# Token-major value products, and six gates and six outputs of the merge's third branch, as pairs of 512 and 256 columns

## The chip, the cores and the metric

One core of one Trainium2 chip. The metric is the device time of one execution, in microseconds (us), on that core. The parts named here are TensorE (PE: matmuls, and PEld: weight loads), VectorE (DVE), ScalarE (ACT), GpSimd (POOL) and SyncE (SP, whose queue issues nearly all DMAs), the on-chip memory SBUF and the matmul accumulators PSUM.

## The reference

Two layers over 256 tokens of width 1024. Each layer is a SwiGLU FFN, a mixer and a second SwiGLU FFN, each behind an RMS norm and added to the residual stream; a norm ends the program. The mixer projects the normed input once and feeds three branches, which a gated merge adds up:

```python
h = rms_norm(x, mix_norm[l])
proj = h @ w_in[l]
gm_u, gm_v, r_q, r_k, r_v, r_g, n_q, n_kv, n_g = jnp.split(proj, splits, axis=-1)
y_a = gmlp_mixer(jax.nn.gelu(gm_u), jax.nn.gelu(gm_v), ...)
y_b = retention_mixer(r_q, r_k, r_v, r_g, ...)
y_c = nsa_mixer(n_q, n_kv, n_g, ...)
g_a, g_b, g_c = jnp.split(jax.nn.sigmoid(h @ w_merge_gate[l] + b_merge_gate[l]), N_MIXERS, axis=-1)
mix = g_a * (y_a @ w_branch_out[l, 0]) + g_b * (y_b @ w_branch_out[l, 1]) + g_c * (y_c @ w_branch_out[l, 2])
x = x + mix @ w_o[l]
```

All data is float32.

## The kernel before

**Splits.** Every large product is done with operands split in two parts, a rounded high part and the rest (low), both of type float32r: high by high, high by low and low by high are accumulated in PSUM. Weights come in pieces of 512 KB through `issue` (lines 197 to 216): SP's queue loads a piece (`raw`, 3 buffers), ScalarE casts it to the high part (line 210), and VectorE and GpSimd subtract to get the low part (line 214), GpSimd taking a share of the columns. The two parts lie in one tile `hl` (4 buffers), so that `wk[k]` is a block of 128 rows with its high and low columns side by side. `piece` (line 220) hands a piece to a product and issues up to AHEAD = 2 pieces further.

**Two ways to multiply.** Feature-major products (features on the output's partitions, 256 tokens along its columns) hold the weight in the array. `mm_feat` (line 231) issues three matmuls of 256 columns for each block of 128 rows ("a step"). `mm_wide` (line 254) issues two for the same step: the weight's high part by the activations' high and low parts side by side, 512 columns into a whole PSUM bank, then its low part by the high activations, 256 columns added to the first half. The bank then holds two halves that have yet to be added. The first FFN product does so for most tiles (its halves are added after a copy by ScalarE, lines 391 and 392), and the second FFN product and the output product do so for seven of eight (they add both halves to x, line 374). Token-major products (tokens on the partitions) hold the activations in the array: `mm_tok` (line 269) issues three matmuls of 256 columns for each step, for one half of the tokens.

**Order.** TensorE's order is the order in which the program writes its matmuls; the products are generators that yield after each step, and `run_sides` lets side jobs (attention units, retention, gmlp, compression) write their instructions in between, when a condition holds or when an estimate of TensorE's time, `clk`, has gone on by so much. The other engines' queues are ordered by the tile framework when the program is built, and its waits are placed there too.

**The mixer** (`mixer`, line 489) runs: four feature-major tiles of keys and values, the token-major keys' and gates' product of 280 columns, queries, retention's queries and keys, then the token-major products that the change touches. `tok` (line 869) is called four times with two pieces of four steps of 256 columns: twice for the gMLP's values (`gv_evac`, line 797) and twice for the retention's values (`f_vr`, line 939). Each call fills one PSUM bank "mm" (2 buffers), one half of the tokens after the other, and then evacuates both halves with two ScalarE copies scaled by the tokens' norm factor `st["r"]`, line 800 or 942. After the second call for the gMLP a side job, `gv_norm` (line 805), applies gelu (`gelu2`, lines 455 to 461: squares and tanh on ScalarE, two VectorE steps at 459 and 461 per token half) and a layer norm. After the second call for the retention's values, `retention` (line 734) goes on: its products with the values wait for line 942. Meanwhile `unit` (line 616) computes attention: score matmuls from the "sc" banks (3 buffers), maxima on VectorE (645, 648), exponentials on ScalarE (650), scaling of P (652 to 655), transposes on TensorE (149).

**The merge.** Gates and branch outputs of branches a and b are done for eight tiles (lines 997 to 1009), interleaved with attention. Then branch c: gates two tiles at a time (`gates`, line 978: one "mm" bank for two gates, multiplication by the norm factor R at line 984, tanh on ScalarE at 987), outputs two tiles at a time (`outs`, line 990, four steps each, one "sc" bank), their gated product at line 1034 on VectorE, its addition to the other branches on GpSimd (1035), and the split of the merged tiles into high and low (`split_mix`, 1016 on ScalarE and 1017 on VectorE) for the output product, which starts with two tiles interleaved (`mm_pair`, line 1051) and needs the merged tiles in order. The last two outputs (d = 6) are done one tile at a time, with their own additions on VectorE (1043, 1045).

Of the kernel before, what the change touches and what calls it, by code (L numbers as in the profile page):

```python
# [9 lines left out]
AF = mybir.ActivationFunctionType  # L10
# [50 lines left out]
def tile_hybrid_block(  # L61
# [48 lines left out]
    def t2(tag="t2", bufs=6):  # L110
        return act.tile([128, 512], F32, tag=tag, name=nm(tag), bufs=bufs)
# [4 lines left out]
    def pmm():  # L116
        return ps.tile([128, 512], F32, tag="mm", name=nm("mm"), bufs=2)

    def psc():
        return ps.tile([128, 512], F32, tag="sc", name=nm("sc"), bufs=3)  # L120
# [17 lines left out]
    def mm(o, lhsT, rhs, start, stop):  # L138
        nc.tensor.matmul(o, lhsT=lhsT, rhs=rhs, start=start, stop=stop)  # L139
        n = 1  # L140
        for d in rhs.shape[1:]:
            n *= d
        if lhsT.dtype == F32R:
            clk[0] += max(n / 2400.0, 0.107) + 0.0025
        else:
            clk[0] += max(4 * n / 2400.0, 0.214)
# [73 lines left out]
    def piece(kn, n, cuts=1, between=None, ahead=AHEAD):  # L220
        if between:
            issue(cuts, between)
        i = used[0]
        while len(queue) < len(specs) and len(queue) <= i + ahead:
            issue({1: 4, 2: 2}.get(len(queue), 1))
        used[0] += 1
        assert specs[i] == (kn, n)
        r, queue[i] = queue[i], None
        return r
# [24 lines left out]
    def mm_wide(o, wk, ak, first, last):  # L254

        n = len(wk)
        for i in range(n):
            mm(o.rearrange("p (a b) -> p a b", a=2), lhsT=wk[i][:, 0], rhs=ak[i], start=first and i == 0, stop=False)
            mm(o[:, 0:256], lhsT=wk[i][:, 1], rhs=ak[i][:, 0], start=False, stop=last and i == n - 1)
            yield  # L260
# [8 lines left out]
    def mm_tok(o, wk, ak, half, first, last):  # L269

        n = len(wk)
        t = slice(half * 128, half * 128 + 128)
        for i in range(n):
            wh, wl = wk[i][:, 0], wk[i][:, 1]
            ah, al = ak[i][:, 0], ak[i][:, 1]
            mm(o, lhsT=ah[:, t], rhs=wh, start=first and i == 0, stop=False)
            mm(o, lhsT=ah[:, t], rhs=wl, start=False, stop=False)
            mm(o, lhsT=al[:, t], rhs=wh, start=False, stop=last and i == n - 1)
            yield


# [81 lines left out]
    def when_scaled(st, f):  # L363
        if "R" in st:
            f()
        else:
            st["q"].append(f)
# [121 lines left out]
    def mixer(l, st, nxt):  # L489
# [304 lines left out]
        u2 = {}  # L794
        vl = []

        def gv_evac(c):
            def f(p):
                for h in range(2):
                    S.activation(vls[:, 512 * h + c * 256:512 * h + c * 256 + 256], p[:, h * 256:h * 256 + 256], AF.Copy, scale=st["r"][:, h:h + 1])  # L800
                if c:
                    side(gv_norm())
            return f

# [64 lines left out]
        def tok(cuts, n, f):  # L869
            if n > 256:  # L870
                ps_ = [psc(), pmm()]
                k = 0
                for m in cuts:
                    wk = piece(m, n)
                    for i in range(m):
                        for h in range(2):
                            yield from mm_tok(ps_[h][:, 0:n], wk[i:i + 1], a[k:k + 1], h, k == 0, k == 7)
                        k += 1
                for h in range(2):
                    when_scaled(st, lambda h=h: f(h, ps_[h]))  # L880
            else:
                wk = []
                for i, m in enumerate(cuts):
                    wk += piece(m, n, ahead=min(AHEAD, 3 - i))
                p = pmm()
                for h in range(2):
                    yield from mm_tok(p[:, h * n:h * n + n], wk, a, h, True, True)
                when_scaled(st, lambda: f(p))

        def f_c(i, o):  # L890
            for n in range(2):
# [45 lines left out]
            ev.add("kr")  # L937

        def f_vr(c):
            def f(p):  # L940
                for h in range(2):
                    S.activation(vr[h][:, c * 256:c * 256 + 256], p[:, h * 256:h * 256 + 256], AF.Copy, scale=st["r"][:, h:h + 1])
                if c:
                    ev.add("vr")
            return f

# [31 lines left out]
        def gates(idx):  # L978
            p = pmm()
            for n, i in enumerate(idx):  # L980
                wk = piece(8, 128)
                yield from mm_feat(p[:, n * 256:n * 256 + 256], wk, a, True, True)
            t = t2("tg", 2)
            V.tensor_tensor(out=t.rearrange("p (a b) -> p a b", a=2), in0=p.rearrange("p (a b) -> p a b", a=2), in1=R2(), op=ALU.mult)
            for n, i in enumerate(idx):
                h = t[:, n * 256:n * 256 + 256]
                S.activation(h, h, AF.Tanh, scale=0.5, bias=bm[:, i:i + 1])
            return t

        def outs(pairs, wks, alloc=pmm):  # L990
            p = alloc()
            for n, (b, d) in enumerate(pairs):
                yield from mm_feat(p[:, n * 256:n * 256 + 256], wks[n], [yt[b][:, :, k] for k in range(4)], True, True)
            return p
# [23 lines left out]

        for d in range(0, 8, 2):
            if d < 6:  # L1020
                t_next = yield from gates((d + 18, d + 19))
            if d == 4:
                mx_["t"] = x16()
                mx_["h"], mx_["l"] = mx_["t"][:, 0], mx_["t"][:, 1]
                split_mix(0, 2)
                split_mix(2, 2)
            if d == 0:
                finish(has("yc0", "yc1"))
            wk = piece(8, 128)
            if d < 6:  # L1030
                p = yield from outs(((2, d), (2, d + 1)), (wk[0:4], wk[4:8]), psc)
                dst = mv_[d // 4][:, d % 4 * 256:d % 4 * 256 + 512]
                u = t2()
                V.scalar_tensor_tensor(u, t_prev, 1.0, p, op0=ALU.add, op1=ALU.mult)
                G.tensor_tensor(out=dst, in0=dst, in1=u, op=ALU.add)
                if d == 4:
                    split_mix(4, 2)
            else:
                u = t2()
                for n in range(2):  # L1040
                    p = yield from outs(((2, d + n),), (wk[4 * n:4 * n + 4],), psc)
                    h = u[:, n * 256:n * 256 + 256]
                    V.scalar_tensor_tensor(h, t_prev[:, n * 256:n * 256 + 256], 1.0, p[:, 0:256], op0=ALU.add, op1=ALU.mult)
                    dst = ms[1][:, 2 + n]
                    V.tensor_tensor(out=dst, in0=dst, in1=h, op=ALU.add)
                    split_mix(d + n, 1)
            t_prev = t_next
# [183 lines left out]
```

## Time and profile before

| | us |
|---|---|
| Median of 3 runs | 1282.31 (1279.55 to 1282.56) |
| Profiled execution, device time | 1278.46 |
| Its span, first to last instruction | 1276.7 |
| TensorE busy | 1252.9 (98%) |
| VectorE busy | 972.6 (76%) |
| ScalarE busy | 714.9 (56%) |
| GpSimd busy | 495.9 (39%) |

The profile is of one execution. Its matmuls are pipelined: a record's length holds the time in the pipeline, so the pace is read from starts. The mixers of the two layers lie at about 199 to 458 and 825 to 1085 us of the span.

### The profile page before, as it was taken

To read this page: it belongs to the slowest core of one execution; us is meant where nothing else is said; L and a number is where in the kernel's file an instruction comes from. 1 tells how busy PE (TensorE), PEld (TensorE's weight loads), DVE (VectorE), ACT (ScalarE), POOL (GpSimd) and SP (SyncE) were. 2 spreads that over 40 slices of the span, in tenths; PEclk is the share of its full clock that TensorE was granted. 3 is DMA by queue.
4 is the path that set the end of the run, shared out by engine and by line. 5 is a ranking of instruction groups with operands and counts; after the bars stand their busy time and mean duration, and the time that the engine had idled before them with its cause. 6 is when DMAs were issued, how large, how long until landed. Compare 5 with 4: busy or idle time off the path is not lost.

```text
span 1276.7 us, 22870 instructions
## 1 busy us (share of the span) xinstructions
PE 1252.9 (98%) x8464; PEld 1152.9 (90%) x8464; DVE 972.6 (76%) x1659; ACT 714.9 (56%) x1209; POOL 495.9 (39%) x459
## 2 busy tenths in 40 slices
PE   9999999999999999999999999999999999999997
PEld 8888889999999988888898888998999999888886
DVE  5888777689875888887778887666997759788764
ACT  4666545466764556665456664455676545566642
POOL 4533121663445743331213322236635558133222
PEclk8999999999999999999999999999999999999999
DMA  7765566754444565555655555666445455665562
GB/s 238 246 202 190 184 188 190 230 173 157 140 151 158 172 190 190 185 193 183 199 184 193 187 189 183 192 205 198 150 127 165 149 153 181 190 188 186 188 194 91
DMA packets 70303, 231.51 MB, mean 181 GB/s; under 512 B 9392, under 2 KB 12080, under 8 KB 70192
## 3 DMA queue, kind: packets, MB, share of 16 engines
q1 hardware_dynamic: 70048, 230.03, 56.6%
q8 instruction: 66, 1.08, 0.4%
q14 instruction: 45, 0.37, 0.1%
q10 hardware_dynamic: 144, 0.03, 0.0%
HBM read 225.80 MB, written 1.05 MB: 178 GB/s over the span
## 4 chain that ended last, share of the span: by engine, by line
PE 81%; DVE 7%; DMA 5%; ACT 3%; issue 2%; POOL 2%; SPq 0%; POOLq 0%; DVEq 0%; ACTq 0%
PE mm L139 56%; PE sc L139 21%; DMA raw<-in_w_dram 4%; DVE hl L214 2%; ACT hl L210 2%; PE o L139 2%; POOL hl L214 2%; PE ms L139 1%; PE sc L149 1%; DVE xhl L315 1%; DMA x<-in_x_dram 0%; ACT P L650 0%; DVE t L459 0%; DVE t L563 0%; POOL sq L329 0%
## 5 line engine op out<-in xcount | busy, mean ns | idle before, releaser
L214 DVE TENSOR_TENSOR hl<-raw,hl 128x896 fp32r<-128x896 f32 (+6 forms) x437 | 488.7, 1120 | 176.1 <-ACT hl L210 174.7
L210 ACT CAST hl<-raw 128x1024 fp32r<-128x1024 f32 (+3 forms) x437 | 442.5, 1016 | 263.8 <-PE mm L139 171.3
L139 PE MATMUL mm<-xhl,hl 128*128 128x256 f32 (+1 forms) x3784 | 567.5, 305 | 4.0 <-DVE hl L214 1.3
L139 PEld LDWEIGHTS mm<-xhl,hl 128*128 128x128 f32 x3784 | 510.4, 191 | 38.9 <-DVE hl L214 2.7
L214 POOL TENSOR_TENSOR hl<-raw,hl 128x128 fp32r<-128x128 f32 (+2 forms) x288 | 345.0, 1200 | 485.8 <-ACT hl L210 461.8
L139 PE MATMUL mm<-s,hl 128*128 128x512 f32 (+1 forms) x1880 | 297.2, 318 | 0.0
L139 PEld LDWEIGHTS mm<-s,hl 128*128 128x128 f32 x1880 | 267.0, 188 | 26.9
L139 PE MATMUL sc<-xhl,hl 128*128 128x256 f32 (+1 forms) x1560 | 274.8, 327 | 0.0
L139 PEld LDWEIGHTS sc<-xhl,hl 128*128 128x128 f32 x1560 | 230.3, 188 | 28.0
L329 POOL TENSOR_TENSOR sq<-x 128x256 f32<-128x256 f32 x43 | 30.0, 701 | 133.7 <-DVE x L374 133.7
L391 ACT COPY t<-sc 128x256 f32<-128x256 f32 x81 | 30.1, 372 | 74.1 <-PE sc L139 74.1
L139 PE MATMUL mm<-hl,xhl 128*128 128x256 f32 (+1 forms) x432 | 62.1, 292 | 1.0 <-POOL hl L214 0.7
L391 ACT COPY t<-mm 128x256 f32<-128x256 f32 x81 | 30.1, 372 | 57.5 <-PE mm L139 57.5
L333 POOL TENSOR_TENSOR acc<-acc,sq 128x256 f32<-128x256 f32 x43 | 60.8, 1414 | 2.5
L139 PEld LDWEIGHTS mm<-hl,xhl 128*128 128x128 f32 x432 | 55.4, 190 | 4.5 <-issue 1.9
L393 DVE TENSOR_TENSOR t<-t,R 128x512 f32<-128x512 f32 x81 | 56.9, 702 | 2.8
L399 ACT ACTIVATE t<-t 128x256 f32<-128x256 f32 x88 | 36.7, 418 | 29.1 <-DVE t L393 27.1
L392 DVE TENSOR_TENSOR t<-sc,t 128x256 f32<-128x256 f32 x81 | 34.3, 423 | 21.1 <-ACT t L391 21.1
L374 DVE SCALAR_TENSOR_TENSOR x<-mm,x 128x256 f32<-128x256 f32 x84 | 35.5, 422 | 15.8 <-PE mm L139 14.5
L650 ACT ACTIVATE P<-P,small 128x128 f32<-128x128 f32 (+1 forms) x64 | 28.6, 448 | 31.5 <-DVE small L648 31.4
L315 DVE SCALAR_TENSOR_TENSOR xhl<-x,gnorm,xhl 128x256 fp32r<-128x256 f32 x48 | 41.6, 877 | 5.2 <-ACT xhl L314 5.2
L402 DVE TENSOR_TENSOR s<-t,s 128x256 fp32r<-128x256 f32 x88 | 38.5, 438 | 0.9
(177 smaller groups left out, 849.1 us busy)
## 6 DMA issues: line engine op xcount, KB each, us to landing
raw<-in_w_dram SPq DMA_DIRECT2D x389, 512.0 KB, 3.5
raw<-in_w_dram SPq DMA_DIRECT2D x32, 384.0 KB, 3.1
raw<-in_w_dram SPq DMA_DIRECT2D x4, 420.0 KB, 2.9
x<-in_x_dram SPq DMA_DIRECT2D x4, 256.0 KB, 4.3
raw<-in_w_dram SPq DMA_DIRECT2D x8, 128.0 KB, 4.0
lng<-in_lnp_dram SPq DMA_DIRECT2D x2, 512.0 KB, 5.5
s<-in_c_alibi_dram SPq DMA_DIRECT2D x2, 512.0 KB, 5.6
ks<-ks SPq DMA_DIRECT2D x4, 256.0 KB, 5.8
```

The lines of the kernel that those rows point to most:

```text
L139: nc.tensor.matmul(o, lhsT=lhsT, rhs=rhs, start=start, stop=stop)
L210: S.copy(hi[:, s_], raw[:, s_])
L214: e.tensor_tensor(out=lo[:, a:b], in0=raw[:, a:b], in1=hi[:, a:b].bitcast(F32), op=ALU.subtract)
L315: V.scalar_tensor_tensor(st["l"][:, k], xs[k], g, st["h"][:, k].bitcast(F32), op0=ALU.mult, op1=ALU.subtract)
L329: (V if last else G).tensor_tensor(out=q, in0=xs[k], in1=xs[k], op=ALU.mult)
L333: (V if last else G).tensor_tensor(out=st["acc"], in0=st["acc"], in1=q, op=ALU.add)
L374: V.scalar_tensor_tensor(xs[d], p[:, i:i + 256], 0.5, xs[d], op0=ALU.mult, op1=ALU.add)
L391: S.copy(t3[:, n], p[n][:, 256:512])
L392: V.tensor_tensor(out=t3[:, n], in0=p[n][:, 0:256], in1=t3[:, n], op=ALU.add)
L393: V.tensor_tensor(out=t3, in0=t3, in1=R2, op=ALU.mult)
L399: S.activation(u[:, 0:256], t[:, 0:256], AF.Silu)
L402: V.tensor_tensor(out=l4[:, j % 4], in0=u[:, 256:512], in1=h4[:, j % 4].bitcast(F32), op=ALU.subtract)
```

## The change

The four `tok` products of 256 columns use a new `mm_tok_wide`: each step is a matmul of 512 columns (high activations by the weight's high and low parts) and one of 256 (low activations by the high part) added to the first half. Each half of the tokens now has a PSUM bank of its own, "sc" for the first and "mm" for the second, and is evacuated as soon as it is done: `tok_evac` copies one half of the bank with ScalarE, scaled by r, and a VectorE scalar_tensor_tensor adds the other half times r. In the merge's third branch, the gates of tiles 18 to 23 and the outputs of tiles 0 to 5 use `mm_wide`, with a bank for each; `join` copies one half with ScalarE and adds the other with VectorE. The gates then are multiplied by R out of SBUF. Line 1034 takes the joined tile from SBUF where it took the PSUM bank. The gates 16 and 17, the outputs of tiles 6 and 7, all of branches a and b, and every other product stay as they are.

```diff
+    def mm_tok_wide(o, wk, ak, half):
+
+        n = len(wk)
+        t = slice(half * 128, half * 128 + 128)
+        for i in range(n):
+            mm(o.rearrange("p (a b) -> p a b", a=2), lhsT=ak[i][:, 0, t], rhs=wk[i], start=i == 0, stop=False)
+            mm(o[:, 0:256], lhsT=ak[i][:, 1, t], rhs=wk[i][:, 0], start=False, stop=i == n - 1)
             yield
...
+        def tok_evac(o, h, p):
+            t = t2()[:, 0:256]
+            r = st["r"][:, h:h + 1]
+            S.activation(t, p[:, 256:512], AF.Copy, scale=r)
+            V.scalar_tensor_tensor(o, p[:, 0:256], r, t, op0=ALU.mult, op1=ALU.add)
+
         def gv_evac(c):
-            def f(p):
-                for h in range(2):
-                    S.activation(vls[:, 512 * h + c * 256:512 * h + c * 256 + 256], p[:, h * 256:h * 256 + 256], AF.Copy, scale=st["r"][:, h:h + 1])
-                if c:
+            def f(h, p):
+                tok_evac(vls[:, 512 * h + c * 256:512 * h + c * 256 + 256], h, p)
+                if c and h:
                     side(gv_norm())
             return f
...
-                p = pmm()
-                for h in range(2):
-                    yield from mm_tok(p[:, h * n:h * n + n], wk, a, h, True, True)
-                when_scaled(st, lambda: f(p))
+                for h, p in enumerate((psc(), pmm())):
+                    yield from mm_tok_wide(p, wk, a, h)
+                    when_scaled(st, lambda h=h, p=p: f(h, p))
...
         def f_vr(c):
-            def f(p):
-                for h in range(2):
-                    S.activation(vr[h][:, c * 256:c * 256 + 256], p[:, h * 256:h * 256 + 256], AF.Copy, scale=st["r"][:, h:h + 1])
-                if c:
+            def f(h, p):
+                tok_evac(vr[h][:, c * 256:c * 256 + 256], h, p)
+                if c and h:
                     ev.add("vr")
             return f
...
+        def join(p, t):
+
+            S.copy(t, p[:, 256:512])
+            V.tensor_tensor(out=t, in0=p[:, 0:256], in1=t, op=ALU.add)
+
+        def gates_wide(idx):
+            t = t2("tg", 2)
+            for n, i in enumerate(idx):
+                p, h = pmm(), t[:, n * 256:n * 256 + 256]
+                yield from mm_wide(p, piece(8, 128), a, True, True)
+                join(p, h)
+                V.tensor_tensor(out=h, in0=h, in1=st["R"], op=ALU.mult)
+                S.activation(h, h, AF.Tanh, scale=0.5, bias=bm[:, i:i + 1])
+            return t
+
+        def outs_wide(pairs, wks):
+            t = t2()
+            for n, (b, d) in enumerate(pairs):
+                p = psc()
+                yield from mm_wide(p, wks[n], [yt[b][:, :, k] for k in range(4)], True, True)
+                join(p, t[:, n * 256:n * 256 + 256])
             return t
...
             if d < 6:
-                t_next = yield from gates((d + 18, d + 19))
+                t_next = yield from gates_wide((d + 18, d + 19))
...
             if d < 6:
-                p = yield from outs(((2, d), (2, d + 1)), (wk[0:4], wk[4:8]), psc)
+                p = yield from outs_wide(((2, d), (2, d + 1)), (wk[0:4], wk[4:8]))
                 dst = mv_[d // 4][:, d % 4 * 256:d % 4 * 256 + 512]
                 u = t2()
                 V.scalar_tensor_tensor(u, t_prev, 1.0, p, op0=ALU.add, op1=ALU.mult)
```

## Rows read from the trace of the kernel before

**Rows 1.** The page, busy us (share of the span) and instructions of each engine.

```profile
PE 1252.9 (98%) x8464; PEld 1152.9 (90%) x8464; DVE 972.6 (76%) x1659; ACT 714.9 (56%) x1209; POOL 495.9 (39%) x459
```

**Rows 2.** Timeline, PE: start us, length us, engine, line, operation, tiles, count [idle before].

```profile
62.47 2.94 PE L139 MATMUL sc<-xhl,hl 128*128 128x512 f32 x16
65.24 2.94 PE L139 MATMUL mm<-xhl,hl 128*128 128x512 f32 x16
...
412.69 5.91 PE L139 MATMUL mm<-xhl,hl 128*128 128x256 f32 x48
418.43 3.00 PE L139 MATMUL sc<-s,hl 128*128 128x256 f32 x24
```

**Rows 3.** Timeline, PE, in the token-major product of the retention's values.

```profile
268.00 5.20 PE L139 MATMUL mm<-hl,xhl 128*128 128x256 f32 x42
```

**Rows 4.** Timeline, PE, in the first token-major product of the gMLP's values.

```profile
247.84 1.95 PE L139 MATMUL mm<-hl,xhl 128*128 128x256 f32 x12 [0.17 <-POOL hl L214]
```

**Rows 5.** Timeline, PE, the retention's products with the values, first and second layer.

```profile
279.77 0.71 PE L139 MATMUL ms<-s,s 128*128 128x128 f32 x4 [1.91 <-ACT s L942]
...
284.17 0.38 PE L139 MATMUL ms<-s,s 128*128 128x128 f32 x2
...
906.95 1.16 PE L139 MATMUL ms<-s,s 128*128 128x128 f32 x4 [1.91 <-ACT s L942]
...
912.90 0.38 PE L139 MATMUL ms<-s,s 128*128 128x128 f32 x2
```

**Rows 6.** Timeline, PE, first score matmul and the wait for line 654, both layers.

```profile
267.73 0.43 PE L139 MATMUL sc<-ks,xhl 128*128 128x288 f32 x2
...
323.60 0.33 PE L149 MATMUL sc<-sq,P 128*128 128x128 f32 x1 [2.07 <-DVE P L654]
...
894.91 0.43 PE L139 MATMUL sc<-ks,xhl 128*128 128x288 f32 x2
...
949.91 0.33 PE L149 MATMUL sc<-sq,P 128*128 128x128 f32 x1 [0.30 <-DVE P L654]
```

**Rows 7.** Windows: stretch, us, busy PE, PEld, DVE, ACT, POOL, granted clock, DMA share, GB/s.

```profile
263.00:323.30 60.30, 56.18 (x462) 55.20 (x461) 56.30 (x156) 41.14 (x91) 30.83 (x28) 1.00 0.47 153
...
278.00:286.00 8.00, 6.23 (x53) 6.23 (x54) 6.72 (x24) 4.85 (x14) 6.89 (x6) 1.00 0.55 179
905.00:913.00 8.00, 6.09 (x38) 6.05 (x38) 6.72 (x24) 4.86 (x13) 6.87 (x6) 0.79 0.34 102
```

**Rows 8.** The chain of waits in 255 to 326: start us, us, what holds it.

```profile
263.63 0.47 ACT s L800
...
265.76 1.72 DVE t L459
...
268.16 1.29 DVE s L461 x2
```

**Rows 9.** Groups of instructions: line, engine, operation, shapes, count, busy us, mean ns, idle before.

```profile
L374 DVE SCALAR_TENSOR_TENSOR x<-mm,x 128x256 f32<-128x256 f32 x84 | 35.5, 422 | 15.8 <-PE mm L139 14.5
...
L391 ACT COPY t<-sc 128x256 f32<-128x256 f32 x81 | 30.1, 372 | 74.1 <-PE sc L139 74.1
...
L984 DVE TENSOR_TENSOR tg<-mm,R 128x512 f32<-128x512 f32 x24 | 16.4, 685 | 10.3 <-PE mm L139 10.3
```

**Rows 10.** Windows, a pair of gates and a pair of outputs of the merge's third branch.

```profile
418.40:427.00 8.60, 8.60 (x74) 8.60 (x73) 5.98 (x6) 4.59 (x6) 6.16 (x5) 1.00 0.61 191
```

**Rows 11.** Timeline, PE and DVE, from the last outputs to the output product.

```profile
427.02 5.84 PE L139 MATMUL sc<-s,hl 128*128 128x256 f32 x48
...
432.70 2.46 PE L139 MATMUL mm<-xhl,hl 128*128 128x256 f32 x18
...
433.06 1.18 DVE L1017 TENSOR_TENSOR xhl<-s,xhl 128x512 fp32r<-128x512 f32 x1
```

**Rows 12.** Timeline, DVE, two weight splits of the same size in the merge.

```profile
419.77 0.82 DVE L214 TENSOR_TENSOR hl<-raw,hl 128x640 fp32r<-128x640 f32 x1 [0.44 <-ACT hl L210]
...
422.60 1.62 DVE L214 TENSOR_TENSOR hl<-raw,hl 128x640 fp32r<-128x640 f32 x1 [0.44 <-ACT hl L210]
```

More of the change, by code (lines that the diff above doesn't have):

```diff
@@ L278, in mm_tok @@
             mm(o, lhsT=al[:, t], rhs=wh, start=False, stop=last and i == n - 1)
+            yield
+    def mm_tok_wide(o, wk, ak, half):
[4 more added lines that the diff above has]
+            mm(o[:, 0:256], lhsT=ak[i][:, 1, t], rhs=wk[i][:, 0], start=False, stop=i == n - 1)
             yield
@@ L988, in gates @@
             return t
+        def join(p, t):
[16 more added lines that the diff above has]
+                join(p, t[:, n * 256:n * 256 + 256])
+            return t
         def outs(pairs, wks, alloc=pmm):
```

## Prediction

> **What bounds the kernel now.** I read the page's busy shares first: TensorE (PE) is busy 98% of the span [rows 1]. So time can only be won where TensorE issues, or where it waits. Second, TensorE's timeline, by starts and not by lengths, since records overlap. A narrow run of 48 matmuls (two pieces, 16 steps of three 256-column matmuls) takes 412.69 to 418.43 in the merge, 0.359 us a step; a pair of 512 and 256 columns, which the first FFN product already uses, takes 2.77 us for 8 steps, 0.346 a step [rows 2]. Token-major matmuls run at the narrow pace: 42 take 0.71 us less than the 48, 0.118 for each one fewer [rows 2, 3]. A step that becomes a pair is thus worth 0.0125 us, wherever TensorE isn't waiting for something else.
>
> Third, where TensorE does wait in the mixer. Inside the first token-major product it waits for GpSimd's (POOL's) share of a weight split [rows 4]. In the retention it waits 1.91 us for the last evacuation of the values (ScalarE (ACT), line 942), in both layers [rows 5]. Some 45 us later it waits for VectorE's (DVE's) scaling of P (line 654): 2.07 us in the first layer, 0.30 in the second [rows 6]. The layers show how these hang together. After the retention's wait, the second layer needs 906.95 to 912.90 up to the next retention matmul, the first 279.77 to 284.17 for the same instructions: 1.55 us more, with the granted clock at 0.79 in 905 to 913 (the 1.2 GHz level for part of it) [rows 5, 7]. Yet the later wait is 1.77 us shorter there, and from the first score matmul to the end of that wait the layers need 55.87 and 55.00 us [rows 6]. What TensorE loses early it doesn't lose again late: something else sets the end of this stretch. The windows say what: VectorE is busy 56.3 of 60.3 us in it [rows 7], and the chain of waits runs on VectorE once the gated values are out of PSUM (line 800), through the gelu (lines 459 and 461) [rows 8].
>
> **The change, part by part.** Per layer, 64 token-major steps become pairs (two products, two column halves, two token halves, eight steps), and in the merge 48 gate steps and 24 output steps. In all 2 x (64 + 72) = 272 steps, 3.4 us of issue. No DMA is added or moved, and the weights arrive as before. The order of the other engines' queues is settled when the program is built, and side work is placed by an estimate of TensorE's time that a pair changes by 0.003 us a step: I can't see the new order, and the spread of the chances is mostly that. What of the 3.4 us arrives?
>
> *Ahead of VectorE's chain.* The chain starts from the end of the gated values. Of their 32 steps the first eight wait for GpSimd anyway [rows 4], so 24 x 0.0125 = 0.3 us a layer comes off. The 32 steps of the retention's values lie beside the VectorE-bound stretch and are costed at nothing; if VectorE weren't the bound there, they would be worth 0.4.
>
> *Token-major evacuation.* Before: eight ScalarE copies of 256 columns a layer, 0.47 us [rows 8]. After: as many, each followed by a VectorE scalar_tensor_tensor (PSUM times r, plus the copy). The nearest row is line 374: the same operation, width and kinds of source, 422 ns [rows 9]. VectorE thus gets 8 x 0.42 = 3.4 us a layer. The first four come before line 459, where VectorE is not on the chain, and the last of them takes the place of a second serial copy there (0.47 against 0.42): nothing. The four of the retention's values, 1.7 us, fall in the bound stretch. Against them: each token half is now evacuated by itself, so the gelu's first half can start 8 steps or 2.8 us earlier, in VectorE's idle time. That takes half of lines 459 and 461 off the chain, (1.72 + 1.29) / 2 = 1.5 [rows 8]. VectorE was also idle 1.28 of the 8 us from 278 [rows 7], partly since ScalarE and TensorE stood in the retention's wait; I credit half, 0.65. Net -0.45 us a layer. Bounds: no relief at all, +1.7; all adds in gaps and all relief, -2.8.
>
> *The retention's wait.* It is for the first token half of the second column half, which will be ready 2.8 us sooner, with one addition behind it. The 1.91 us should go. By the reading above TensorE then meets line 654 that much earlier and waits there instead: 0, with a gain of 1.91 a layer and 1.55 once for the clock as the other end. I take 0: the two layers side by side are the nearest thing to this experiment that the trace holds. What stands behind the new additions on VectorE's queue are the score maxima (line 645) and line 648, for which ScalarE's exponentials wait, and behind those line 654, for which TensorE waits.
>
> *The merge's third branch.* Issue: 72 x 0.0125 = 0.9 us a layer; TensorE has no wait here. ScalarE gets 12 copies of 0.37; VectorE gets 12 additions and, for three multiplications by R at 0.69, six of half the width, all at 0.42 (by line 374) [rows 9]: per pair of tiles 6 x 0.42 - 0.69 = 1.8 us, so 7.8 us of some 8.5, where it had 5.98 of 8.6 [rows 10]. Weight splits run two pieces (AHEAD), 5.7 us, ahead, which hides that load; with the cover gone TensorE would wait for splits, up to 1 us a layer. The two "mm" buffers of PSUM are each refilled 5.5 us after their gate ended, and copy and addition need about 1.
>
> One chain has no room: the last wide pair's outputs (d = 4) feed line 1034, GpSimd's line 1035, the split of the merged tiles and then the output product. Now the outputs end near 429.86 (half of 427.02 to 432.70), the split ends at 433.06 + 1.18 = 434.24, and TensorE wants these tiles 12 matmuls after 432.70, at 434.14 [rows 11]. The edge is already touched. The join puts a copy (0.37), an addition (0.42) and a handover (0.06) into it: 0.85 us of new wait a layer. Merge in all: -0.05 a layer.
>
> Something in the rows speaks against this part. VectorE's operations that read PSUM keep their length: line 374 averages 422 ns over 84 of them, line 984 685 ns over 24 [rows 9]. A weight split on VectorE, with both inputs in SBUF, took 0.82 us at 419.77 and 1.62 at 422.60, where GpSimd was in line 1035 [rows 12]. Line 1034 read PSUM and will read two SBUF tiles; behind a GpSimd instruction it would be late by some 0.8 us, as that split was. The Trainium skill (SBUF — State Buffer, "Who interferes with whom") says so outright: a VectorE instruction with two SBUF inputs and a GpSimd one that reads SBUF exclude each other for their whole length, one with a single SBUF input is free. By that rule, the rows agreeing, any overlap costs. I take no overlap, since GpSimd's own line 1035 waits for line 1034; the other case is a rival.
>
> *Sum:* 2 x (-0.3 - 0.45 - 0.05) = -1.6 us. The profiled execution took 1278.46 (span 1276.7 and 1.8 around it), so 1276.9 in its terms; the median of the runs shown lies 3.85 higher, and 1282.3 - 1.6 = **1280.7**.
>
> **The rivals.** *VectorE is not the bound (faster).* Line 654 is late merely through its place in the queue, and another order frees it. Then 3.4 of issue, the two retention waits (3.8) and the clock's 1.55 come off, less 1.7 for the output product's chain: -7; with the first layer's later wait half kept, about -5.5: 1276.8. For it: weight splits have slack and could stand further back. Against it: 93% busy, and the equal sums of the layers.
>
> *VectorE falls further behind (slower).* None of the four retention adds finds a gap and the gelu's early half isn't taken: +1.7 a layer, against -0.3 and -0.05. And the waits merge into one of over 2 us at line 654, after which the clock falls as it did at 907. That fall lay in VectorE's cover; one behind line 654 doesn't: +1.55 in one layer or in both. 2 x 1.35 + 1.55 to 3.1 = +4.3 to +5.8: about 1287. It decides once the adds delay lines 645 and 648 by over 1 us. For it: only 4 us idle in 60. Against: the first adds come before the chain, where VectorE has room.
>
> *GpSimd in the way of line 1034.* +0.8 a layer at the output product: 1282.3. It decides if GpSimd's next split is queued ahead of line 1035.
>
> *The pair does nothing here.* The stationary operand is now activations, and no such pair is in the trace. Then the 0.6 and 1.8 us counted for issue stay: 1283.1. As both operand orders run at one pace now, I leave it inside the forecast's own range.
>
> **How the numbers follow.** Forecast 0.36, GpSimd in the way 0.12, VectorE not the bound 0.32, VectorE further behind 0.20. A measurement of this kernel can tell about 0.3%, 3.85 us, from no change. Forecast and GpSimd's case lie within it: same 0.48; faster 0.32; slower 0.20. The forecast's own range is 1278 to 1284. The whole range has to reach into both outer cases: down to 2 x (-0.3 - 2.8 - 0.05) = -6.3 and a little of the clock, up to the slower case: **1275.5 to 1287.0**.
>
> **What would show it.** Pairs in the token-major and merge stages start 2.77 us per 8 steps apart; the wait on the values' evacuation is gone from the retention; the wait for line 654 is 2 us or more in both layers; the output product's first tile waits about 1 us for line 1017. The forecast is wrong if the wait for line 654 stays as it was while the retention's is gone (faster), if a lowered clock follows line 654 (slower), or if line 1034 takes over a microsecond (GpSimd in the way).

## The result and the profile after

The change makes the kernel slower: 1292.12 us (1290.14 to 1293.79, 4 runs) against 1281.17 us (1279.55 to 1282.56, 4 runs), a ratio of 1.0089 with a 95% interval of 1.0075 to 1.0103. The forecast was 1280.7 us, with a range up to 1287.0. The profiled execution took 1291.20 us with a span of 1289.4, 12.7 more than the profiled one before; 2.5 of these are there by the first token-major product of the mixer (keys' and gates', 211.70 and 214.22), up to which both kernels are alike.

The line numbers of the changed kernel are higher: 654 is now 663, 1034 and 1035 are 1069 and 1070, 1016 and 1017 are 1051 and 1052, 1043 and 1045 are 1078 and 1080. New are the token evacuation (809 on ScalarE, 810 on VectorE), the joins (copy 1004, addition 1005) and the product by R at half width (1013). In the kernels of the experiments, lines behind an edit lie up to five higher.

The page's busy times answer to [rows 1]: 272 matmuls fewer, and TensorE is still busy for longer.

```profile
PE 1256.1 (97%) x8192; PEld 1140.4 (88%) x8192; DVE 992.7 (77%) x1705; ACT 721.3 (56%) x1233; POOL 491.2 (38%) x459
```

TensorE's timeline in the token-major products, the retention and the attention of the first layer, then the attention of the second, answers to [rows 3, 5, 6].

```profile
265.88 2.94 PE L139 MATMUL sc<-hl,xhl 128*128 128x512 f32 x16
268.66 1.89 PE L139 MATMUL mm<-hl,xhl 128*128 128x512 f32 x10
270.39 0.43 PE L139 MATMUL sc<-ks,xhl 128*128 128x288 f32 x2
...
280.68 0.71 PE L139 MATMUL ms<-s,s 128*128 128x128 f32 x4 [0.31 <-DVE s L810]
...
297.14 0.33 PE L149 MATMUL sc<-sq,P 128*128 128x128 f32 x1 [1.69 <-DVE P L663]
...
326.62 0.33 PE L149 MATMUL sc<-sq,P 128*128 128x128 f32 x1 [2.66 <-DVE P L663]
...
900.73 0.42 PE L139 MATMUL sc<-ks,xhl 128*128 128x288 f32 x2
...
956.30 0.44 PE L149 MATMUL sc<-sq,P 128*128 128x128 f32 x1 [2.13 <-DVE P L663]
```

A window behind that last wait (the columns of [rows 7]):

```profile
957.00:961.00 4.00, 4.00 (x25) 4.00 (x25) 3.56 (x12) 3.23 (x9) 0.58 (x2) 0.65 0.70 244
```

Eight token-major steps take 2.78 us (265.88 to 268.66), the forecast pace of a pair. The retention's wait fell from 1.91 to 0.31 us, and the waits for line 663 grew. From the first score matmul to the end of the later wait it is 56.23 us (270.39 to 326.62) and 55.57 us (900.73 to 956.30), where it was 55.87 and 55.00 [rows 6]. The second layer's fall of the clock has moved: it stood behind the retention's wait (0.79 in 905 to 913 [rows 7]) and stands behind line 663's now (0.65 in 957 to 961). From the first layer's merge to the second layer's last attention output it is 593.1 us in both kernels. This half of the change gives nothing and takes little.

The loss is in the merge. From the last matmul that makes branch c's attention output to the first update of x it takes 38.13 us in the first layer (408.07 to 446.20) and 38.04 in the second; before, 33.19 in both (405.06 to 438.25 in the first). Twice 4.9 is 9.8 us, and the medians lie 10.95 apart. TensorE's timeline there, answering to [rows 2, 11]:

```profile
415.51 5.72 PE L139 MATMUL mm<-xhl,hl 128*128 128x512 f32 x32
...
423.88 5.72 PE L139 MATMUL mm<-xhl,hl 128*128 128x512 f32 x32
429.44 4.39 PE L139 MATMUL sc<-s,hl 128*128 128x512 f32 x28
437.01 2.50 PE L139 MATMUL sc<-s,hl 128*128 128x256 f32 x12 [3.18 <-DVE t L1005]
439.31 2.48 PE L139 MATMUL mm<-xhl,hl 128*128 128x256 f32 x13
442.13 0.86 PE L139 MATMUL mm<-xhl,hl 128*128 128x256 f32 x5 [0.34 <-DVE xhl L1052]
```

A pair of gates and a pair of outputs take 8.37 us (415.51 to 423.88), as forecast. Then the last output (tile 7) waits 3.18 us for an addition of line 1005: it wants an "sc" bank, of which there are three. Tiles 4 and 5, wide, hold one each (narrow, they shared one), tile 6 holds the third, and tile 4's is free only when its two halves are joined. The same matmul waits 3.16 us in the second layer. Behind the wait TensorE is slow, as the windows say (the columns of [rows 7]):

```profile
433.70:437.00 3.30, 0.13 (x2) 0.00 (x0) 3.17 (x6) 1.86 (x5) 0.99 (x1) 1.00 0.50 153
437.00:442.10 5.10, 4.78 (x25) 4.58 (x25) 4.67 (x7) 2.09 (x3) 2.85 (x2) 0.67 0.63 202
```

A mean clock of 0.67 over 5.1 us is 3.4 us at the 1.2 GHz level, which costs TensorE half of that, 1.7. But the waits and the clock are not separate causes to be added up. The matmul at 442.13 waits for the split of tiles 4 and 5, whose last part runs on VectorE (its timeline):

```profile
441.38 0.69 DVE L1052 TENSOR_TENSOR xhl<-s,xhl 128x512 fp32r<-128x512 f32 x1 [0.40 <-ACT xhl L1051]
```

It ends 34.0 us behind the start of this stretch (442.07 and 408.07); before, it ended 29.2 behind it (434.24 and 405.06 [rows 11]). From there to the update of x it is 4.1 us, 4.0 before. So these 4.8 us are the loss, and the wait for the bank and the slow clock lie inside them. It builds up pair by pair: the splits of the three pairs of tiles end 13.3, 23.7 and 34.0 us behind the start, where they ended 12.0, 20.6 and 29.2. That is 1.3 us with the first pair, 1.8 with the second and 1.7 with the third.

Why are the joins and splits late? Tile 4's matmuls ended near 430.8 (half of the 16 from 429.44). Its copy ran at 436.15. The other engines' timelines between the copies of tiles 2 and 3 and those of tiles 4 and 5:

```profile
425.79 0.63 ACT L1004 COPY t<-sc 128x256 f32<-128x256 f32 x2
...
430.41 0.62 ACT L1051 CAST xhl<-s 128x512 fp32r<-128x512 f32 x1 [3.04 <-POOL s L1070]
430.93 0.37 ACT L1004 COPY tg<-mm 128x256 f32<-128x256 f32 x1
...
433.00 0.35 ACT L1004 COPY tg<-mm 128x256 f32<-128x256 f32 x1
...
435.73 0.51 ACT L1014 ACTIVATE tg<-tg,bm 128x256 f32<-128x256 f32 x1 [1.44 <-DVE tg L1013]
436.15 0.62 ACT L1004 COPY t<-sc 128x256 f32<-128x256 f32 x2
...
426.17 0.76 DVE L1005 TENSOR_TENSOR t<-sc,t 128x256 f32<-128x256 f32 x2
426.96 0.69 DVE L1069 SCALAR_TENSOR_TENSOR t<-tg,t 128x512 f32<-128x512 f32 x1
...
432.12 0.42 DVE L1013 TENSOR_TENSOR tg<-tg,R 128x256 f32<-128x256 f32 x1
432.46 1.64 DVE L214 TENSOR_TENSOR hl<-raw,hl 128x640 fp32r<-128x640 f32 x1
434.03 0.41 DVE L1005 TENSOR_TENSOR tg<-mm,tg 128x256 f32<-128x256 f32 x1
434.47 1.23 DVE L1013 TENSOR_TENSOR tg<-tg,R 128x256 f32<-128x256 f32 x1
...
427.50 1.03 POOL L214 TENSOR_TENSOR hl<-raw,hl 128x384 fp32r<-128x384 f32 x1 [2.44 <-ACT hl L210]
428.50 1.87 POOL L1070 TENSOR_TENSOR s<-s,t 128x512 f32<-128x512 f32 x1
```

This is a loop through three queues. The copies of outputs 2 and 3 (425.79) lead to their joins and to line 1069 (426.96). GpSimd's add for them stands behind GpSimd's share of a weight split, and ends at 430.37, 2.72 us after line 1069. ScalarE's split of those tiles has waited 3.04 us for it, and **behind that waiting split stands the copy of gate 22**, whose matmuls had ended near 426.7. Gate 22's join, its product by R, a weight split, gate 23's join and product by R follow on VectorE. ScalarE waits 1.44 us for the last of these with the tanh of gate 23, and behind that tanh stand the copies of outputs 4 and 5 (436.15). From 425.79 to 436.15 is 10.36 us; TensorE needs 8.37. The program writes the split of tiles 0 and 1 and that of 2 and 3 behind the gates of d = 4; the framework queued each ahead of a gate's copy.

Before, the same split also waited for GpSimd, but for 1.00 us, as GpSimd's and ScalarE's timelines of the kernel before show:

```profile
422.24 1.30 POOL L1035 TENSOR_TENSOR s<-s,t 128x512 f32<-128x512 f32 x1 [0.78 <-DVE t L1034]
...
423.57 0.62 ACT L1016 CAST xhl<-s 128x512 fp32r<-128x512 f32 x1 [1.00 <-POOL s L1035]
```

GpSimd's add then stood ahead of its next weight share: in all six cases it began 0.08 us after the end of line 1034 and ended 1.3 us later. In the changed kernel the share stands first in all six: the add begins 0.83 or 0.84 us after line 1069 and ends 2.67 to 2.72 us after it.

And ScalarE freed no bank of PSUM in this branch then: VectorE read the gates and the outputs itself, so nothing that TensorE wanted stood behind.

### The profile page after: what moved, and what is told of

It reads as the page before. It is cut to its first block, busy times and chain, and to the rows that moved or that the text cites. A ratio compares the mean times of both kernels' runs of the same rounds, so it can differ in the third digit from the quotient of the medians.

```text
span 1289.4 us, 22408 instructions
## 1 busy us (share of the span) xinstructions
PE 1256.1 (97%) x8192; PEld 1140.4 (88%) x8192; DVE 992.7 (77%) x1705; ACT 721.3 (56%) x1233; POOL 491.2 (38%) x459
## 5 line engine op out<-in xcount | busy, mean ns | idle before, releaser
L210 ACT CAST hl<-raw 128x1024 fp32r<-128x1024 f32 (+3 forms) x437 | 443.0, 1016 | 238.5 <-PE mm L139 156.9
L214 POOL TENSOR_TENSOR hl<-raw,hl 128x128 fp32r<-128x128 f32 (+2 forms) x288 | 337.5, 1173 | 507.7 <-ACT hl L210 479.6
L401 DVE TENSOR_TENSOR t<-mm,t 128x256 f32<-128x256 f32 x81 | 34.3, 423 | 6.7 <-ACT t L400 1.4
L410 ACT CAST s<-t 128x256 fp32r<-128x256 f32 x88 | 35.8, 406 | 4.3 <-DVE t L409 4.3
```

What stands on the lines that cost most here:

```text
L210: S.copy(hi[:, s_], raw[:, s_])
L214: e.tensor_tensor(out=lo[:, a:b], in0=raw[:, a:b], in1=hi[:, a:b].bitcast(F32), op=ALU.subtract)
L401: V.tensor_tensor(out=t3[:, n], in0=p[n][:, 0:256], in1=t3[:, n], op=ALU.add)
L410: S.copy(h4[:, j % 4], u[:, 256:512])
```

## The experiments

### The parts alone

**e1_token**: the token-major pairs alone, the merge as before.

```diff
-                t_next = yield from gates_wide((d + 18, d + 19))
+                t_next = yield from gates((d + 18, d + 19))
-                p = yield from outs_wide(((2, d), (2, d + 1)), (wk[0:4], wk[4:8]))
+                p = yield from outs(((2, d), (2, d + 1)), (wk[0:4], wk[4:8]), psc)
```

> The token-major pairs alone; the merge's third branch as before. Theory A (the merge's evacuation chain costs nearly all): within 2 us of the kernel before, as the landmarks of the two traces give +0.5 us for the first layer's token-major stretch and 0 for the second's; the retention's wait of 1.9 us is gone and the waits for the scaling of P add up to 3 to 5 us a layer. Theory B (VectorE's extra adds in the bound stretch cost a good part): slower than before by 3 us or more.

Measured: 1280.14 us against 1279.95, ratio 1.0002 [0.9989, 1.0015]. The merge stage is 33.18 us in both layers. TensorE's timeline shows the retention's wait gone and the first wait for line 663 grown as with the whole change; the later one is shorter here:

```profile
279.67 0.71 PE L139 MATMUL ms<-s,s 128*128 128x128 f32 x4 [0.40 <-DVE s L810]
...
296.26 0.33 PE L149 MATMUL sc<-sq,P 128*128 128x128 f32 x1 [1.82 <-DVE P L663]
...
325.15 0.33 PE L149 MATMUL sc<-sq,P 128*128 128x128 f32 x1 [0.84 <-DVE P L663]
```

The two add up to 2.66 us in the first layer, under the 3 to 5 expected, and to 3.66 in the second.

**e2_merge**: the merge's pairs alone. `tok` multiplies with `mm_tok` into one "mm" bank and evacuates with one scaled ScalarE copy for each half, as before.

```diff
-                for h, p in enumerate((psc(), pmm())):
-                    yield from mm_tok_wide(p, wk, a, h)
-                    when_scaled(st, lambda h=h, p=p: f(h, p))
+                q = pmm()
+                for h in range(2):
+                    yield from mm_tok(q[:, h * n:h * n + n], wk, a, h, True, True)
+                for h in range(2):
+                    when_scaled(st, lambda h=h: f(h, q[:, h * n:h * n + n]))
```

> The merge's pairs alone; token-major products with three matmuls, one bank and scaled ScalarE copies as before. Theory A: slower than before by 8 to 11 us, with a wait of about 3.2 us of the last outputs for a bank and a lowered clock behind it in both layers. Theory B: slower by 6 us or less.

Measured: 1288.8 us, ratio 1.0066 [1.0051, 1.0082]. The wait for the bank is there in full (TensorE's timeline):

```profile
435.79 1.69 PE L139 MATMUL sc<-s,hl 128*128 128x256 f32 x12 [3.16 <-DVE t L1007]
```

**e3_gates** is that kernel with the six outputs narrow (`outs` in place of `outs_wide`), **e4_outs** with the six gates narrow (`gates` in place of `gates_wide`).

> Only the six gates a layer as pairs; outputs and token-major products as before. Two outputs share a bank again, so the last outputs never wait for one. Theory A in its form 'a bank short': no slower than before, -1 to +1 us. Theory A in its form 'the copy-add-multiply-tanh chain falls behind and everything after it is late': slower by 2 to 8 us, the wait moving to the output product's split tiles.

> Only the six outputs a layer as pairs; gates and token-major products as before. 'A bank short': the last outputs wait for the bank of tile 4, but its join is only one copy and one add away, so 0 to 1 us a layer: 0 to +2 us in all. 'The chain falls behind': the gates' part is missing, so the join's 0.85 us a layer of the record's own working shows at the output product: +0.5 to +2 us. Both put most of the loss in having gates and outputs together or in the gates.

Measured: gates alone 1279.7 us, ratio 0.9995 [0.9985, 1.0005]; outputs alone 1281.39 us, ratio 1.0012 [1.0002, 1.0022]. Neither has the bank's wait. Wide outputs alone wait at the output product, where the forecast had put 0.85 us, and the merge stage takes 34.78 us in the first layer and 34.72 in the second:

```profile
436.87 0.38 PE L139 MATMUL mm<-xhl,hl 128*128 128x256 f32 x1 [0.77 <-ACT xhl L1053]
437.60 0.87 PE L139 MATMUL mm<-xhl,hl 128*128 128x256 f32 x5 [0.34 <-DVE xhl L1054]
```

Of 1280 us the ratios are +0.3 for the token part, -0.6 for gates and +1.5 for outputs, but +8.4 for gates and outputs together. So the loss is neither's own; it needs both. The traces show a part of each: with wide outputs alone GpSimd's add begins behind a share in all six cases, 0.83 to 0.88 us after the gated product, and with wide gates alone it begins 0.08 us after it; ScalarE's copies of gates, behind which the loop runs on, are there with wide gates only.

### What closes the loop

Two readings were left: a bank is missing, or the queues fall behind and the bank is merely where TensorE meets it. A third reading, that VectorE is simply full, has to be told from the second: it is busy 8.31 of the 10.35 us from 425.80 to 436.15. Five kernels, each the changed kernel with one or two edits, tell them apart.

**e5_bank**: tile 7 gets a bank that is free.

```diff
-                    p = yield from outs(((2, d + n),), (wk[4 * n:4 * n + 4],), psc)
+                    p = yield from outs(((2, d + n),), (wk[4 * n:4 * n + 4],), pmm if n else psc)
```

> The changed kernel, but the outputs of tile 7 go into one of the two mm banks in place of the third sc bank. Nothing else is touched, and ScalarE's queue is the same. Theory 'a bank short': the changed kernel loses its 4.9 us a layer because the wide outputs take a bank for each tile where the narrow ones took one for two, so that tile 7 has none. Then the 3.2 us wait and the lowered clock behind it go, and the time is 7 to 10 us below the changed kernel. Theory 'the queues fall behind': the bank is only where TensorE meets the late join of tile 4. Then tile 7 starts 3.2 us earlier, and TensorE waits for as long at the output product instead, first for the bank that its second accumulator shares with tile 4 or for the split of tiles 4 and 5 (line 1052, done at 442.1 now): 0 to 2 us below the changed kernel, merge stage 36.5 to 38 us.

Measured: 1293.92 us, ratio 1.0108 [1.009, 1.0126], not better than the changed kernel. Tile 7 no longer waits, and TensorE waits 4.70 us later on (its timeline, then a window):

```profile
434.42 1.58 PE L139 MATMUL mm<-s,hl 128*128 128x256 f32 x12
435.84 1.59 PE L139 MATMUL mm<-xhl,hl 128*128 128x256 f32 x12
442.12 2.17 PE L139 MATMUL mm<-xhl,hl 128*128 128x256 f32 x6 [4.70 <-ACT xhl L1051]
```

```profile
444.00:448.00 4.00, 4.00 (x21) 4.00 (x20) 1.85 (x3) 0.41 (x1) 0.81 (x1) 0.50 0.38 131
```

The bank theory falls. The merge's matmuls resume at 442.12, as they did at 442.13, since the split of tiles 4 and 5 comes no sooner: it ends 34.0 us behind the stage's start here too. The merge stage is even longer, 40.28 and 39.34 us, since the 1.2 GHz level behind the longer wait now lies behind that split and is no longer covered by it.

**e6_late**: the two splits are queued behind the copies of the next two outputs. **e8_latebank** has both edits.

```diff
-            S.copy(t, p[:, 256:512])
+            last[0] = S.copy(t, p[:, 256:512]).ins
...
-                split_mix(0, 2)
-                split_mix(2, 2)
+                with tc.issue_after(last_o[0]):
+                    split_mix(0, 2)
...
+                last_o[0] = last[0]
                 if d == 4:
-                    split_mix(4, 2)
+                    with tc.issue_after(last_o[0]):
+                        split_mix(2, 2)
+                        split_mix(4, 2)
```

> The changed kernel, but the splits of tiles 0 and 1 and of tiles 2 and 3 (line 1051 on ScalarE) are queued behind the copies of the next two outputs. They stand ahead of the next gate's copy now, and wait 3.0 us there for GpSimd's add. Theory 'the queues fall behind', in its form 'a loop through in-order queues' (copy of an output, join, line 1069, GpSimd's weight share and add, split, copy of the gate, its products, tanh, copy of the next output: 10.36 us a pair where TensorE needs 8.4): without that link the copies keep up with TensorE, the 3.2 us wait falls to under 0.5, and the output product waits 0.5 to 1.5 us for splits that now come later: 5 to 9 us below the changed kernel. Theory 'VectorE is full': it is busy 8.3 us of a pair with GpSimd holding back its two-input work, so that TensorE still waits 1.5 us or more for the bank: 0 to 4 us below. Theory 'a bank short': no change.

> The two edits together: splits queued behind the copies, and tile 7 in an mm bank. If the loop was the cause, the bank adds nothing to the later splits: within 1.5 us of the kernel with later splits alone, and about the time of the kernel before or up to 2 us below it. If both were needed, it is over 3 us below that kernel.

Measured: 1283.42 us, ratio 1.0021 [1.001, 1.0032], and with the bank 1283.16 us, 1.0022 [1.0012, 1.0032]. The time of the kernel before, expected of the second, is not reached. Some 8.7 us of the 11 come back by the place of the splits in the queues alone (line 1051 on ScalarE and, with it, 1052 on VectorE), and the bank adds nothing. ScalarE now copies gate 22 when it is done, and TensorE has one wait left, at the output product:

```profile
425.26 0.62 ACT L1053 CAST xhl<-s 128x512 fp32r<-128x512 f32 x1
426.87 0.37 ACT L1004 COPY tg<-mm 128x256 f32<-128x256 f32 x1 [0.99 <-PE mm L139]
...
437.98 0.86 PE L139 MATMUL mm<-xhl,hl 128*128 128x256 f32 x5 [1.06 <-DVE xhl L1054]
```

**e7_addv**: the add of line 1070 leaves GpSimd.

```diff
-                G.tensor_tensor(out=dst, in0=dst, in1=u, op=ALU.add)
+                V.tensor_tensor(out=dst, in0=dst, in1=u, op=ALU.add)
```

> The changed kernel, but the add of line 1070 (tiles 0 to 5 of the merged branch) runs on VectorE, right behind line 1069, in place of GpSimd. Theory 'loop through in-order queues': GpSimd's weight share (1.03) and its add (1.87) leave the loop, VectorE's 0.7 to 1.5 us come in, so the pair takes some 8.5 to 9 us, the bank wait falls from 3.2 to about 1 us, and the time is 3 to 8 us below the changed kernel. Theory 'VectorE is full': VectorE gets 0.7 to 1.5 us more a pair, 9.0 to 9.8 us, and the time is no better, or 1 to 3 us worse.

Measured: 1281.91 us, ratio 1.0017 [1.0006, 1.0028], 9 us below the changed kernel by the ratios, though VectorE has more to do; so VectorE being full was not the cause. What is left is again mostly at the output product (TensorE's timeline):

```profile
433.91 1.69 PE L139 MATMUL sc<-s,hl 128*128 128x256 f32 x12 [0.19 <-DVE t L1005]
...
437.26 0.38 PE L139 MATMUL mm<-xhl,hl 128*128 128x256 f32 x1 [0.24 <-ACT xhl L1051]
438.28 0.86 PE L139 MATMUL mm<-xhl,hl 128*128 128x256 f32 x5 [0.64 <-DVE xhl L1052]
```

**e9_nopool**: GpSimd takes no share of the weight splits in this branch.

```diff
+        pool_lo[0] = 8
         for d in range(0, 8, 2):
...
+        pool_lo[0] = MIX_SPLIT
         nst = norm_begin(nxt)
```

> The changed kernel, but GpSimd takes no share of the weight splits in the loop of the third branch: VectorE subtracts all 1024 columns, where it had 640 and GpSimd 384. GpSimd keeps its add of line 1070. Theory 'GpSimd holds the loop' (its share of 1.03 us queued ahead of its add, VectorE's subtraction at 1.64 instead of 0.82 and the product by R at 1.23 instead of 0.42 while it runs): the products by R all take 0.42, the add starts right behind line 1069, the loop of 10.36 us loses some 2 us or more, the bank wait of 3.2 falls to under 1 and the time is 4 to 10 us below the changed kernel, though VectorE subtracts more. Theory 'VectorE's load alone': 384 columns more for each piece are 0.5 us, 1.5 a pair, and the wait stays at 3 us or grows.

Measured: 1284.72 us, ratio 1.0036 [1.0023, 1.0048], 7 us below the changed kernel. The split still stands ahead of gate 22's copy and still waits for GpSimd, but every product by R takes 0.42 us, and from copy to copy (420.67, behind a split as here, to 429.59) it is 8.92 us where it was 10.39 (420.54 to 430.93):

```profile
429.06 0.62 ACT L1051 CAST xhl<-s 128x512 fp32r<-128x512 f32 x1 [2.82 <-POOL s L1071]
429.59 0.37 ACT L1004 COPY tg<-mm 128x256 f32<-128x256 f32 x1
...
432.70 0.42 DVE L1013 TENSOR_TENSOR tg<-tg,R 128x256 f32<-128x256 f32 x1
...
426.82 2.21 POOL L1071 TENSOR_TENSOR s<-s,t 128x512 f32<-128x512 f32 x1 [6.71 <-DVE t L1070]
...
434.65 1.69 PE L139 MATMUL sc<-s,hl 128*128 128x256 f32 x12 [0.26 <-DVE t L1005]
```

What is left is at the output product again, 1.29 and 0.34 us in the first layer.

Three different cuts into the loop (the split's place, the add, GpSimd's share) each take the 3.2 us wait down to 0.3 or less, and each brings the split of tiles 4 and 5 forward: it ends 29.9 us (e6_late), 30.3 (e7_addv) and 31.1 (e9_nopool) behind the stage's start, where it was 34.0. With any of these three links shortened the copies keep up.

### What the pairs can give

**e10_tokgates** leaves the six outputs narrow. **e11_best** has the add on VectorE and only the outputs of d = 4 narrow, so that no join stands ahead of the output product.

```diff
-                p = yield from outs_wide(((2, d), (2, d + 1)), (wk[0:4], wk[4:8]))
+                o = (outs_wide, ()) if d < 4 else (outs, (psc,))
+                p = yield from o[0](((2, d), (2, d + 1)), (wk[0:4], wk[4:8]), *o[1])
```

> The changed kernel with the six outputs as before, narrow: token-major products and the six gates are pairs. By the sum of the single parts (token 0.2, gates -0.6 us against the kernel before): -0.4 us, ratio 0.9985 to 1.001. If wide gates and wide token products disturb each other as gates and outputs do, it is over 2 us slower.

> The changed kernel with line 1070's add on VectorE and the last pair of outputs (tiles 4 and 5) narrow, so that no join stands in the chain ahead of the output product. The loop theory expects no bank wait, less than 0.5 us of wait at the output product and a merge stage of 32.6 to 33.2 us (33.19 before): ratio 0.998 to 1.0005, at best 2 us faster than the kernel before. If the chain ahead of the output product was not what is left of the loss in the kernel with the add on VectorE, it stays 1 to 2 us slower than before.

Measured: 1279.91 us, ratio 0.9997 [0.9989, 1.0006], and 1280.34 us, ratio 1.0002 [0.9989, 1.0015], against 1280.54 before. In the second, TensorE has no wait left here in the first layer (timeline; then the window of the output product):

```profile
437.74 2.39 PE L139 MATMUL mm<-xhl,hl 128*128 128x256 f32 x18
```

```profile
434.00:442.00 8.00, 8.00 (x68) 7.97 (x68) 7.97 (x12) 4.07 (x7) 3.61 (x4) 1.00 0.70 193
```

Its merge stages are 32.48 and 32.90 us where they were 33.19, so the issue time arrives there, 1.0 us in all. That is less than these runs can tell from nothing. No version was clearly faster than the kernel before.

## Why the prediction was wrong

**The step that failed** is the merge's evacuation: "Weight splits run two pieces (AHEAD), 5.7 us, ahead, which hides that load", and "the two 'mm' buffers of PSUM are each refilled 5.5 us after their gate ended, and copy and addition need about 1". Each evacuation was costed as if it began when its matmuls ended. What the runs showed in its place: a gate's copy began 4.2 us after its matmuls (426.7 to 430.93), behind a split that waited for GpSimd, and the loop of copies took 10.36 us to TensorE's 8.37. A lag of 2.0 us a pair grows, by the end of the branch, into the 3.2 us wait. The sentence also speaks of the "mm" banks only; the "sc" banks, where the wait appeared, were not counted. That miscount hid the place and not the cause, as e5_bank shows. VectorE's load I summed (7.8 of 8.5), but the chain that runs from queue to queue I did not.

**A second sum in that step was off.** The products by R were priced at 0.42 by a row that reads PSUM [rows 9]. They read two SBUF tiles, and four of the twelve took 1.22 to 1.26 us; each of these began 0.03 to 0.05 us after GpSimd began a share of a split, and none of the other eight began while one ran. Without that share all took 0.42 (e9_nopool). The Trainium skill's rule (SBUF — State Buffer, "Who interferes with whom") is that a VectorE instruction with two SBUF inputs contends with a GpSimd one that reads SBUF. The trace agrees with it at these instructions, and I applied it to line 1034 only.

**GpSimd in the way of line 1034**: the condition that the prediction gave came true, the effect was another. GpSimd's share is queued ahead of its add (line 1070) in all six cases. But line 1069 is done by then and keeps its 0.69 us (it took 1.40 at d = 4 in e7_addv, where it began beside a share). It is the add that ends 1.3 us later behind line 1069 than it did behind 1034. The prediction put 0.8 us a layer on this, at the output product; it fell on every pair, as a link of the loop.

**The pair's pace**: right, 2.78 us for eight steps. The rival that a pair does nothing with activations in the array is false.

**Ahead of VectorE's chain, and the token evacuation**: -1.5 us forecast over both layers, +0.3 measured (e1_token, -1.4 to +1.9). The forecast lies just outside that interval, on the hopeful side.

**The retention's wait**: right. It went, and the two waits for line 663 in the first layer took it up: 1.69 + 2.66, where there had been 0.43 and 2.07. So of the two outer rivals "VectorE is not the bound" is false. "VectorE falls further behind" is not the cause either: the token part alone costs nothing that these runs can tell. Its sign, a lowered clock behind that line, did show in the second layer (0.65 in 957 to 961), but the one behind the retention's wait had gone. The later wait in the first layer is no firm number: in single profiled executions it lay between 0.8 and 2.7 us with the new token code (0.84 in e1_token), and with the old one it was 2.07 in the kernel before and 0.76 in e3_gates. What decides that is open, and the prediction's reading of two layers of one execution stood on it in part.

**The chain ahead of the output product**: right in kind and too small: +0.85 forecast, 0.77 + 0.34 us of waiting in e4_outs, where the split of tiles 4 and 5 ends 1.5 us later behind the stage's start (30.65 for 29.18). With e11_best, where that join is taken out, the wait is gone in the first layer and 0.29 us in the second.

**The slower rivals** had a mechanism each, at line 654 (now 663) and at line 1034 (now 1069). Neither followed the third branch's queues round to TensorE, so the range ended at 1287.0, below the measured 1292.12.

## What to carry to other kernels

When an evacuation moves to another engine, write down that engine's queue around it, in order, and follow what each instruction ahead of it waits for: a wait that cost nothing while only weight casts stood behind it becomes TensorE's wait once a PSUM copy does. Then add up the whole loop, from one evacuation through all queues to the next of its kind, and compare that with TensorE's time for the same work; busy shares of 47 to 80% on these three engines said nothing about it here. Two parts of a change that each cost little alone can close such a loop together, so measure them alone and together.

## What the hardware showed beyond that

GpSimd's add of 512 columns (line 1035, now 1070) has no fixed length: 1.3 us in all six cases before; 1.85 to 1.88 in the changed kernel, where it began behind GpSimd's share while VectorE's part of the same split was still running (427.57 to 429.21); and 2.21 in four of six cases in e9_nopool, where it started beside a VectorE subtraction of 1024 columns that took 1.22, as its neighbours did. And the clock can be lower behind a wait: behind 3.18 us of waiting the granted clock was 0.67 for 5.1 us, behind 4.70 us it was 0.50 in 444 to 448 (e5_bank), and behind 1.06 us (e6_late) it stayed at 1.00 in 436 to 448. The wait's length alone does not tell: in the changed kernel it was 0.65 in 957 to 961 behind 2.13 us, and 1.00 in 326 to 332 behind 2.66. Nor is a slow clock always a loss: in the changed kernel it lay in the cover of the late split, in e5_bank behind it.
